# Decaying keys and queries in place by block exponents in a chunk-free gated linear attention, with operand packing and mask conversion on other engines

## The chip, the cores and the metric

One core of a Trainium2 chip runs the whole layer as one program. The engines have queues of their own, worked in order: PE (matmul), DVE (vector), ACT (scalar), POOL (GpSimd), and SP, which issues DMAs; POOL and ACT issue DMAs too. The metric is the device time of one execution in microseconds. The kernel before has a median of 878.82 us over three runs (877.24, 878.82, 879.69).

## The reference

A decoder layer on 512 tokens of width 1024: gated linear attention (GLA, 4 heads, keys of 128, values of 256) and multi-head latent attention (MLA, 8 heads) side by side, merged by gates, then an MLP of width 4096. Each half ends in a layer norm. All in float32. What the change touches is the GLA core, here as a recurrence over tokens t, for one head:

```
log_a = log_sigmoid(a_lr @ w_gla_a2 + b_gla_a2) / 16
b     = cumsum(log_a)                            # along the tokens, per channel d
score[i, j] = sum_d q[i, d] * k[j, d] * exp(b[i, d] - b[j, d])     for j <= i
o[i]  = sum_j score[i, j] * v[j]
```

The reference does this in chunks of 64 with a carried state; the result is the same lower triangle of scores over all 512 tokens.

## The kernel before

All matmuls of float32 operands are split in a high and a low part (`split`, and `pump` for weights at L199 and L200): ACT rounds the high part, DVE subtracts it from the source to get the low part, and PE runs three products (hi hi, hi lo, lo hi). Weights come through SP's queue as `wraw`, some through POOL's queue as `wq` with an accumulating DMA. PE is fed by long GEMM loops; between their steps `tick` advances small generators (`active`), whose instructions so fall between the matmuls. A scheduler in the tile framework then orders each engine's queue by its own timing model; `issue_after` pins an instruction behind another.

The order of the work around the change: input layer norm (`ln_in0`, `ln_in1`), the latent projections, `prep` (rope tables and masks), `gemm_fm` for q and k, `latents` (the gate logs GL, one tile per head, channels on partitions, tokens along the row) and `latents2` (RMS norm, transposes), `proj_v(0)`, `proj_r`, `proj_v(1)`, then the gates. From `proj_v(0)` on two generators run beside: `lane_levels` (`gla_levels` for each head) and `lane_out` (`gla_out`).

`gla_levels` builds the triangle of scores by levels s = 1, 2, 4, ..., 256. At level s the tokens are cut in blocks of 2s; the left half's keys meet the right half's queries. A key is decayed to the end of its half, a query from the start of its half. The tokens of the second 256 run backwards, so that `halves` gives left halves of one half and right halves of the other in one view. The steps before:

- `rp` holds two running sums for a head, R (for keys, zero at the start) and G (a copy of GL). `advance(s)` (L846, L847) adds, on POOL, the last value of the neighbour half to the halves: two additions of 128x256 a level.
- `vec(s)` takes E = exp(R / 16) and exp(G / 16) on ACT (L861, two a level), and multiplies them on DVE with the original keys and queries into M (L862, two a level).
- level 1 is done with the diagonal: `q1` (L883), `xs` (L887, L888), four products 192 wide (L897), then L905 (diagonal by the identity) and L906 (predicated copy of level 1).
- L912, L916 and L920 are the matmuls of the levels up to 64, of 128 and of 256, on M. `take` writes a level's scores into SD under a mask (L872, `copy_predicated`); the two largest levels are split for PE directly.
- at the end sd is split, its low part on POOL (L930).

The masks `lmask` are bytes, made by 14 casts on DVE (L566) from the integer tiles `lmi`; the second of these is loaded by `lm_load`: a memset on POOL and seven DMAs in POOL's queue. GL gets its last subtraction on POOL (L657). `ev_k` moves k from PSUM on DVE (L590), and `rms_T` scales the latents on DVE (L607). `latents` also casts aT (L634), which PE needs for the gate logits z (L639); `h_early` adds hraw (L1149).

Of the kernel before, what the change touches and what calls it, by code (L numbers as in the profile page):

```python
# [52 lines left out]
def tile_hybrid_block(ctx: ExitStack, tc: tile.TileContext, I, out, dbg=None):  # L53
# [45 lines left out]
        return bass.AP(tensor=ap.tensor, offset=ap.offset + step * (n - 1), ap=dims[:-1] + [[-step, n]])  # L99

    def view(ap, off, *dims):
        return bass.AP(tensor=ap.tensor, offset=ap.offset + off, ap=[list(ap.ap[0])] + [list(d) for d in dims if d[1] > 1])

    act = nc.scalar.activation
    vtt = nc.vector.tensor_tensor
# [332 lines left out]
    def ln_rows(src, dst, mv, on_act=False, behind=None):  # L438
        bst = S([P, 2, 6], F32, "bst")
        for j in range(2):  # L440
            with ExitStack() as gates:
                if j and behind is not None:
                    gates.enter_context(tc.issue_after(behind.ins))
                nc.vector.bn_stats(bst[:, j, :], src[:, j * T:(j + 1) * T])
        nc.vector.bn_aggr(mv, bst)
        vts(mv[:, 1:2], mv[:, 1:2], LN_EPS, None, op0=ALU.add)  # L446
        gtt(mv[:, 1:2], mv[:, 1:2], mhalf[:, 0:1], op=ALU.pow)  # L447
# [75 lines left out]
    def prep():  # L523
        with tc.issue_after(last_in.ins):
            vts(hbg, bgt, 0.5, None, op0=ALU.mult)
        posf = consts.tile([P, NT], F32, name="posf")
        with tc.issue_after(last_in.ins):
            nc.vector.tensor_copy(posf, posi)
        yield
        p = PX()  # L530
        nc.tensor.transpose(p[:2, :P], posf[:, 2:], identJ)
        nc.tensor.transpose(p[:, P:2 * P], masks[:, P:2 * P], ident)
        pr = B([2, P], F32, "pr")
        nc.vector.tensor_copy(pr, p[:2, :P])
# [24 lines left out]
        yield  # L559
        act(sn, angs[0], AF.Sin)  # L560
        act(cs, angs[1], AF.Sin)
        yield
        for s in LEVELS:
            for d in range(2):
                src = lmi[d][:, LEVELS.index(s), ::s]
                nc.vector.tensor_copy(lm(s)[:, d], src[:, None].to_broadcast([P, 2, 64 // s]))  # L566
        yield


# [17 lines left out]
        act(QK[a][:, 1, :], ps, AF.Copy, scale=P ** -0.5)  # L587

    def ev_k(a, ps):
        nc.vector.tensor_copy(QK[a][:, 0, :], ps)  # L590

    qlT, ckT, qld, ckd, GL, KKs = [], [], [], [], [], []
    aT = B([80, T], F32R, "aT")
# [2 lines left out]
    def rms_T(c0, n, g, outs, rest):  # L596
# [7 lines left out]
        gtt(rs, ss, mhalf[:, :NT], op=ALU.pow)  # L604
        yield
        for tt in range(NT):
            vts(lat[tt][:, c0:c0 + n], lat[tt][:, c0:c0 + n], rs[:, tt:tt + 1], None, op0=ALU.mult)  # L607
        yield
        for k in range(n // P):
            p = PX()  # L610
# [11 lines left out]
    def latents():  # L622
# [31 lines left out]
                last = act(azs[h], azs[h], AF.Ln, bias=1.0)  # L654
        t_ln[0] = last
        for h in range(GH):
            gtt(GL[h], GL[h], azs[h], op=ALU.subtract)  # L657
        yield

    def latents2():  # L660
# [25 lines left out]
        KKs.append(KK)  # L686


    def halves(v, s, right, off=0):

        if s >= P:
            return view(v, off + s * right, (256, T // (2 * s)), (1, s))
        return view(v, off + s * right, (256 - s if right else 256 + s, 2), (2 * s, P // s), (1, s))

    def last(v, s, right):

        if s >= P:
            return view(v, 2 * s - 1 if right else s - 1, (129, T // (2 * s))).to_broadcast([P, T // (2 * s), s])
        o = view(v, 2 * s - 1 if right else s - 1, (257 - 2 * s if right else 257, 2), (2 * s, P // s))
        return o[:, :, :, None].to_broadcast([P, 2, P // s, s])  # L700

    Vh = [[] for _ in range(GH)]
# [130 lines left out]
    def gla_levels(h):  # L833
        qk = QK[h]
        QK[h] = None
        rp = A([P, 2, T], F32, "rp")
        act(rp[:, 1, :], GL[h], AF.Copy)
# [5 lines left out]
        R, G = rp[:, 0, :], rp[:, 1, :]  # L843

        def advance(s):
            gtt(halves(R, s, 0), halves(R, s, 0), last(G, s, 1), op=ALU.add)  # L846
            gtt(halves(G, s, 1), halves(G, s, 1), last(G, s, 0), op=ALU.add)  # L847

        def vec(s):
            E = B([P, T], F32, "E")  # L850
            M = B([P, T], F32, "M")
            for w, src in enumerate((R, G)):
                if s >= P:
                    e, m = [v[:, 256 * w:256 * w + 256].rearrange("p (d i) -> p d i", i=s) for v in (E, M)]
                    if s == 256:
                        e, m = e[:, 0], m[:, 0]
                elif w:
                    e, m = [v[:, 256:].rearrange("p (d n i) -> p d n i", d=2, i=s) for v in (E, M)]
                else:
                    e, m = [v[:, :256].rearrange("p (n d i) -> p d n i", d=2, i=s) for v in (E, M)]  # L860
                act(e, halves(src, s, w), AF.Exp, scale=1.0 / 16.0)  # L861
                vtt(m, e, halves(qk[:, w, :], s, w), op=ALU.mult)  # L862
            if s < 256:
                advance(s)
            return M

        def take(s, p):
# [14 lines left out]
        q1 = B([P, NT, 64], F32, "q1")  # L882
        act(q1.rearrange("p (d t) n -> p d (t n)", d=2), halves(G, 1, 1), AF.Exp, scale=1.0 / 16.0)  # L883
        xs = [B([P, 2, 192], F32, "x1") for _ in range(2)]
        for i in range(2):
            t2 = slice(2 * i * P, 2 * (i + 1) * P)
            act(xs[i][:, :, :P], qk[:, 1, t2].rearrange("p (t i) -> p t i", i=P), AF.Copy)  # L887
            vtt(xs[i][:, :, P:], q1[:, 2 * i:2 * i + 2, :],  # L888
                qk[:, 1, t2].rearrange("p (t n two) -> p t n two", t=2, two=2)[:, :, :, 1 - i], op=ALU.mult)
        advance(1)  # L890
        yield
        px1 = []
        for i in range(2):
            p = PX()
            for t in range(2):
                c = slice((2 * i + t) * P, (2 * i + t + 1) * P)
                mm(p[:, t * 192:(t + 1) * 192], qk[:, 0, c], xs[i][:, t, :], start=True, stop=True)  # L897
            px1.append(p)
        s = 2
        M = vec(2)  # L900
        yield
        for i, p in enumerate(px1):
            pt = p[:, :384].rearrange("p (t c) -> p t c", c=192)
            d = SD[:, 2 * i:2 * i + 2, :]
            vtt(d, pt[:, :, :P], ident[:, None, :].to_broadcast([P, 2, P]), op=ALU.mult)  # L905
            nc.vector.copy_predicated(d.rearrange("p t (n two) -> p t n two", two=2)[:, :, :, 1 - i], lm(1)[:, i], pt[:, :, P:])  # L906
        prev = None
        while s < T:
            p = PX()
            if s <= 64:  # L910
# [14 lines left out]
            if s < T:  # L925
                M = vec(s)
# [820 lines left out]
```

## Time and profile before

| | |
|---|---|
| median of three runs | 878.82 us |
| profiled execution, its own time | 878.11 us |
| its span in the profile | 876.3 us |
| PE busy | 852.6 us (97%), 4711 records |
| DVE busy | 648.5 us (74%), 1093 |
| ACT busy | 470.4 us (54%), 830 |
| POOL busy | 198.6 us (23%), 235 |
| granted PE clock, mean | 0.998 |
| DMA moved | 134.79 MB, mean 154 GB/s |

Busy times count what an engine executes, not register, branch, semaphore or DMA-issuing instructions. Matmuls overlap, so a busy PE can still be a little below its peak. A row of the groups view gives line, engine, operation, output tile and input tiles, shape and count, then the busy time and the mean of one, then the idle time of that engine just before them and what ended it. A row of the waits view gives who waited, for whom, and the sum, the count and the longest.

### The profile page before, as it was taken

The numbers are of one execution on the slowest core, as the hardware profiler recorded it, in microseconds if no ns is written. First come the engines' busy times: TensorE is split into PE (matmuls) and PEld (weight loads), VectorE is DVE, ScalarE is ACT, GpSimd is POOL, SyncE is SP. The second block draws the span as 40 slices with busy tenths as digits, with TensorE's granted clock in tenths as the row PEclk, the third lists the DMA queues.
The fourth block names the chain that finished last, engine by engine and source line by source line (L and its number), as shares of the span: only waits on it lengthen the run. The fifth ranks groups of instructions, "written<-read, shape, count | busy, mean of one in ns | idle before, by whom it ended". The sixth has DMA issues, their size and how long they took to land.

```text
span 876.3 us, 12888 instructions
## 1 busy us (share of the span) xinstructions
PE 852.6 (97%) x4711; PEld 745.0 (85%) x4711; DVE 648.5 (74%) x1093; ACT 470.4 (54%) x830; POOL 198.6 (23%) x235
## 2 busy tenths in 40 slices
PE   5999999999999999999999999999999999999996
PEld 5987887879999978888888889988888888889985
DVE  7869989989665646757876888986567556787865
ACT  5456766756466634436655414576357446666820
POOL 1333536755201030300000013004400520141000
PEclk9999999999999999999999999999999999999999
DMA  7986936694748453322127436007932890499312
GB/s 244 277 190 173 341 121 152 207 264 158 190 115 203 127 149 102 103 65 73 57 83 262 160 121 240 1 1 212 275 90 46 261 246 24 92 238 227 122 61 79
DMA packets 95727, 134.79 MB, mean 154 GB/s; under 512 B 13073, under 2 KB 58564, under 8 KB 95664
## 3 DMA queue, kind: packets, MB, share of 16 engines
q1 hardware_dynamic: 73840, 92.36, 33.1%
q0 software_dynamic: 19616, 37.95, 20.2%
q10 hardware_dynamic: 2208, 3.66, 1.2%
q8 instruction: 37, 0.61, 0.3%
q14 instruction: 26, 0.21, 0.1%
HBM read 110.35 MB, written 8.91 MB: 136 GB/s over the span
## 4 chain that ended last, share of the span: by engine, by line
PE 86%; DVE 8%; DMA 3%; issue 1%; ACT 1%; POOL 0%; POOLq 0%; SPq 0%; DVEq 0%; ACTq 0%
PE mm L255 10%; PE mm L256 10%; PE mm L257 10%; PE mm L291 5%; PE mm L290 4%; PE mm L289 4%; PE mm L1268 4%; PE mm L1266 4%; PE mm L1267 4%; PE px L1556 2%; PE px L1557 2%; PE px L1555 2%; DVE M L862 2%; PE mm L1556 2%; PE mm L1557 2%; PE mm L1555 2%
## 5 line engine op out<-in xcount | busy, mean ns | idle before, releaser
L200 DVE TENSOR_TENSOR wlo<-wraw,whi 128x1024 fp32r<-128x1024 f32 (+1 forms) x102 | 100.5, 994 | 78.1 <-ACT whi L199 73.9
L199 ACT ACTIVATE whi<-wraw 128x1024 fp32r<-128x1024 f32 (+1 forms) x102 | 86.5, 860 | 86.1 <-PE mm L256 47.7
L256 PE MATMUL mm<-h,whi 128*128 128x512 f32 x224 | 87.2, 389 | 0.0
L255 PE MATMUL mm<-h,whi 128*128 128x512 f32 x224 | 87.1, 390 | 0.0
L257 PE MATMUL mm<-h,wlo 128*128 128x512 f32 x224 | 83.3, 390 | 1.6 <-DVE wlo L200 1.6
L1574 POOL DMA_DIRECT2D res<-ev x42 | 36.9, 1007 | 179.1 <-ACT ev L1572 147.8
L200 DVE TENSOR_TENSOR wlo<-wq,whi 128x1024 fp32r<-128x1024 f32 x44 | 55.1, 1252 | 28.1 <-ACT whi L199 28.1
L199 ACT ACTIVATE whi<-wq 128x1024 fp32r<-128x1024 f32 x44 | 46.5, 1057 | 28.9 <-PE mm L1267 20.3
L257 PEld LDWEIGHTS mm<-h,wlo 128*128 128x128 f32 x224 | 42.0, 188 | 10.6 <-DVE wlo L200 2.0
L1268 PE MATMUL mm<-sh,wlo 128*128 128x256 f32 x176 | 50.0, 284 | 0.0
L1267 PE MATMUL mm<-sh,whi 128*128 128x256 f32 x176 | 49.9, 283 | 0.0
L1266 PE MATMUL mm<-sh,whi 128*128 128x256 f32 x176 | 49.9, 283 | 0.0
L256 PEld LDWEIGHTS mm<-h,whi 128*128 128x128 f32 x224 | 42.1, 188 | 8.7
L255 PEld LDWEIGHTS mm<-h,whi 128*128 128x128 f32 x224 | 42.1, 188 | 8.7
L199 ACT ACTIVATE xh<-wraw 128x1024 fp32r<-128x1024 f32 (+1 forms) x28 | 27.2, 985 | 28.4 <-PE mm L291 16.2
L447 POOL TENSOR_TENSOR mv<-mv,mhalf 128x1 f32<-128x1 f32 x4 | 4.7, 1180 | 158.1 <-DVE mv L446 158.1
L862 DVE TENSOR_TENSOR M<-E,qk 128x256 f32<-128x256 f32 x64 | 37.6, 616 | 0.2 <-ACT E L861 0.2
L200 DVE TENSOR_TENSOR xl<-wraw,xh 128x1024 fp32r<-128x1024 f32 (+1 forms) x28 | 31.3, 1127 | 8.8 <-ACT xh L199 8.8
L1620 ACT ACTIVATE relu<-mm 128x512 f32<-128x512 f32 x24 | 14.1, 595 | 41.9 <-PE mm L257 41.9
L846 POOL TENSOR_TENSOR rp<-rp 128x256 f32<-128x256 f32 x32 | 30.3, 946 | 24.8 <-ACT E L861 15.1
L1028 POOL DMA_DIRECT2D QS<-q x32 | 16.0, 507 | 85.1 <-DMA wraw<-in_w_o_gla_dram 48.5
L861 ACT ACTIVATE E<-rp 128x256 f32<-128x256 f32 x64 | 25.8, 418 | 16.4 <-POOL rp L846 9.3
(489 smaller groups left out, 2805.8 us busy)
## 6 DMA issues: line engine op xcount, KB each, us to landing
wraw<-in_w_ff_dram SPq DMA_DIRECT2D x36, 512.0 KB, 5.0
wraw<-in_w_in_dram SPq DMA_DIRECT2D x30, 512.0 KB, 4.8
wq<-in_w_ff_dram POOLq DMA_DIRECT2D x26, 512.0 KB, 9.5
res<-ev POOLq DMA_DIRECT2D x42, 256.0 KB, 10.0
wq<-in_w_in_dram SPq DMA_DIRECT2D x20, 512.0 KB, 6.9
wq<-in_w_in_dram POOLq DMA_DIRECT2D x18, 512.0 KB, 9.5
hsd<-hs SPq DMA_DIRECT2D x16, 256.0 KB, 4.4
xr<-hsd SPq DMA_DIRECT2D x16, 256.0 KB, 4.3
```

The lines of the kernel that those rows point to most:

```text
L199: st["ins"] = act(hi[:, k, :n], raw[:, k, :n], AF.Copy)
L200: st["lo"] = vtt(lo[:, k, :n], raw[:, k, :n], f(hi[:, k, :n]), op=ALU.subtract)
L255: mm(o, hi[:, c], xh, start=first, stop=False)
L256: mm(o, hi[:, c], xl, start=False, stop=False)
L257: mm(o, lo[:, c], xh, start=False, stop=last)
L289: mm(o, xh, hi[:, :n], start=opens, stop=False, skip_group_check=share)
L291: mm(o, xl, hi[:, :n], start=False, stop=last, skip_group_check=share)
L862: vtt(m, e, halves(qk[:, w, :], s, w), op=ALU.mult)
L1266: mm(oa, hi[:, k, c], xh, start=opens and k == 0 and a == 0, stop=False, skip_group_check=True)
L1267: mm(oa, hi[:, k, c], xl, start=False, stop=False, skip_group_check=True)
L1268: mm(oa, lo[:, k, c], xh, start=False, stop=k == 3, skip_group_check=True)
L1574: nc.gpsimd.dma_start(res[tt + t][:, j * T:(j + 1) * T], e, accum_op=ALU.add)
```

## The change

- `gla_levels` keeps no running sums. e1 = exp(GL / 16). The sums of GL over blocks of 2, 4, ..., 256 tokens come from seven halving additions on DVE (256, 128, ..., 4 columns), and one exponential e2 over all of them. K (the tile of the keys itself) and Q (a new tile, q times e1) are decayed in place: at each level ACT copies the left halves of K and the right halves of Q into M, and DVE multiplies these same halves in K and Q by the block exponents of the neighbour half, repeated along the block by the view `across`.
- Level 1 runs as a level like the others (`vec(1)`), and the diagonal is a product of 128 columns by itself, masked by the identity in one operation. At level 128 the matmul reads K and Q directly, and ACT scales one block of each in place for level 256, which reads them directly too.
- Moved: the low part of sd and the subtraction of GL from POOL to DVE; the evacuation of k and the scaling of the latents from DVE to ACT; the mask casts from DVE to POOL, behind the last layer-norm power there; `lm_load` to the front of `prep`.
- `halves` and `view` lose the cases that are no longer used; `last` goes.

The core of the diff:

```diff
     def prep():
         with tc.issue_after(last_in.ins):
             vts(hbg, bgt, 0.5, None, op0=ALU.mult)
+        lm_load()
+        last_pow = st["pow"]
...
-        lm_load()
-        yield
...
-                nc.vector.tensor_copy(lm(s)[:, d], src[:, None].to_broadcast([P, 2, 64 // s]))
+                with tc.issue_after(last_pow.ins):
+                    nc.gpsimd.tensor_copy(lm(s)[:, d], src[:, None].to_broadcast([P, 2, 64 // s]))
...
     def ev_k(a, ps):
-        nc.vector.tensor_copy(QK[a][:, 0, :], ps)
+        act(QK[a][:, 0, :], ps, AF.Copy)
...
-            vts(lat[tt][:, c0:c0 + n], lat[tt][:, c0:c0 + n], rs[:, tt:tt + 1], None, op0=ALU.mult)
+            act(lat[tt][:, c0:c0 + n], lat[tt][:, c0:c0 + n], AF.Copy, scale=rs[:, tt:tt + 1])
...
-            gtt(GL[h], GL[h], azs[h], op=ALU.subtract)
+            vtt(GL[h], GL[h], azs[h], op=ALU.subtract)
...
+    def across(e, s, right):
+        o = view(e, 1 - right, (256 // s + 1 if right else 256 // s - 1, 2), (2, P // s))
         return o[:, :, :, None].to_broadcast([P, 2, P // s, s])
...
     def gla_levels(h):
-        rp = A([P, 2, T], F32, "rp")
-        act(rp[:, 1, :], GL[h], AF.Copy)
-        nc.gpsimd.memset(rp[:, 0, :], 0.0)
+        K, Q = qk[:, 0, :], B([P, T], F32, "QD")
+        e1, sums, e2 = [B([P, T], F32, n) for n in ("e1", "sums", "e2")]
...
-        def advance(s):
-            gtt(halves(R, s, 0), halves(R, s, 0), last(G, s, 1), op=ALU.add)
-            gtt(halves(G, s, 1), halves(G, s, 1), last(G, s, 0), op=ALU.add)
+        def of(v1, v2, s):
+            return v1 if s == 1 else v2[:, T - 1024 // s:T - 512 // s]
...
         def vec(s):
-            E = B([P, T], F32, "E")
             M = B([P, T], F32, "M")
...
-                act(e, halves(src, s, w), AF.Exp, scale=1.0 / 16.0)
-                vtt(m, e, halves(qk[:, w, :], s, w), op=ALU.mult)
-            if s < 256:
-                advance(s)
+            e = of(e1, e2, s)
+            act(M[:, :256].rearrange("p (n d i) -> p d n i", d=2, i=s), halves(K, s, 0), AF.Copy)
+            vtt(halves(K, s, 0), halves(K, s, 0), across(e, s, 0), op=ALU.mult)
+            act(M[:, 256:].rearrange("p (d n i) -> p d n i", d=2, i=s), halves(Q, s, 1), AF.Copy)
+            vtt(halves(Q, s, 1), halves(Q, s, 1), across(e, s, 1), op=ALU.mult)
             return M
...
+        act(e1, GL[h], AF.Exp, scale=1.0 / 16.0)
+        for s in (1, 2, 4, 8, 16, 32, 64):
+            v = of(GL[h], sums, s).rearrange("p (n two) -> p n two", two=2)
+            vtt(of(None, sums, 2 * s), v[:, :, 0], v[:, :, 1], op=ALU.add)
+        act(e2[:, :T - 4], sums[:, :T - 4], AF.Exp, scale=1.0 / 16.0)
+        vtt(Q, qk[:, 1, :], e1, op=ALU.mult)
+        p = PX()
+        for tt in range(NT):
+            c = slice(tt * P, (tt + 1) * P)
+            mm(p[:, c], qk[:, 0, c], qk[:, 1, c], start=True, stop=True)
+        M = vec(1)
+        yield
+        vtt(SD, p.rearrange("p (t c) -> p t c", c=P), ident[:, None, :].to_broadcast([P, NT, P]), op=ALU.mult)
...
             elif s == 128:
                 for i in range(2):
-                    mm(p[:, i * P:(i + 1) * P], M[:, i * P:(i + 1) * P],
-                       M[:, 256 + i * P:256 + (i + 1) * P], start=True, stop=True)
+                    mm(p[:, i * P:(i + 1) * P], K[:, 2 * i * P:(2 * i + 1) * P],
+                       Q[:, (2 * i + 1) * P:(2 * i + 2) * P], start=True, stop=True)
+                e = of(e1, e2, s)
+                act(K[:, :P], K[:, :P], AF.Copy, scale=e[:, 1:2])
+                act(Q[:, 3 * P:], Q[:, 3 * P:], AF.Copy, scale=e[:, 2:3])
             else:
                 for j in range(2):
-                    mm(p[:, j * 256:(j + 1) * 256], M[:, j * P:(j + 1) * P], M[:, 256:], start=True, stop=True)
+                    mm(p[:, j * 256:(j + 1) * 256], K[:, j * P:(j + 1) * P], Q[:, 256:], start=True, stop=True)
+            if s < 64:
+                M = vec(2 * s)
...
         act(sd[:, 0], SD, AF.Copy)
-        gtt(sd[:, 1], SD, f(sd[:, 0]), op=ALU.subtract)
+        vtt(sd[:, 1], SD, f(sd[:, 0]), op=ALU.subtract)
```

More of the change, by code (lines that the diff above doesn't have):

```diff
@@ L101, in view @@
     def view(ap, off, *dims):
-        return bass.AP(tensor=ap.tensor, offset=ap.offset + off, ap=[list(ap.ap[0])] + [list(d) for d in dims if d[1] > 1])
+        return bass.AP(tensor=ap.tensor, offset=ap.offset + off, ap=[list(ap.ap[0])] + [list(d) for d in dims])
     act = nc.scalar.activation
@@ L446, in ln_rows @@
         vts(mv[:, 1:2], mv[:, 1:2], LN_EPS, None, op0=ALU.add)
-        gtt(mv[:, 1:2], mv[:, 1:2], mhalf[:, 0:1], op=ALU.pow)
+        st["pow"] = gtt(mv[:, 1:2], mv[:, 1:2], mhalf[:, 0:1], op=ALU.pow)
         if on_act:
@@ L686, in latents2, with halves @@
         KKs.append(KK)
[L689 to L699, printed above, removed]
+    def halves(v, s, right):
+        return view(v, s * right, (256 - s if right else 256 + s, 2), (2 * s, P // s), (1, s))
+    def across(e, s, right):
+        o = view(e, 1 - right, (256 // s + 1 if right else 256 // s - 1, 2), (2, P // s))
         return o[:, :, :, None].to_broadcast([P, 2, P // s, s])
@@ L841, in gla_levels @@
         s128 = s256 = None
-        R, G = rp[:, 0, :], rp[:, 1, :]
-        def advance(s):
-            gtt(halves(R, s, 0), halves(R, s, 0), last(G, s, 1), op=ALU.add)
-            gtt(halves(G, s, 1), halves(G, s, 1), last(G, s, 0), op=ALU.add)
+        def of(v1, v2, s):
+            return v1 if s == 1 else v2[:, T - 1024 // s:T - 512 // s]
         def vec(s):
-            E = B([P, T], F32, "E")
             M = B([P, T], F32, "M")
[L852 to L862, printed above, removed]
-            if s < 256:
-                advance(s)
+            e = of(e1, e2, s)
[3 more added lines that the diff above has]
+            vtt(halves(Q, s, 1), halves(Q, s, 1), across(e, s, 1), op=ALU.mult)
             return M
@@ L879, in take @@
                 split(p.rearrange("p (a b) -> p a b", b=256), s256[:, 0], s256[:, 1])
[L882 to L890, printed above, removed]
-        yield
[L892 to L907, printed above, removed]
+        act(e1, GL[h], AF.Exp, scale=1.0 / 16.0)
[9 more added lines that the diff above has]
+        M = vec(1)
+        yield
+        vtt(SD, p.rearrange("p (t c) -> p t c", c=P), ident[:, None, :].to_broadcast([P, NT, P]), op=ALU.mult)
+        prev, s = None, 1
         while s < T:
@@ L924, in gla_levels @@
             s *= 2
-            if s < T:
-                M = vec(s)
             yield
```

## The prediction

> **What bounds the kernel now.** First the page's span line and the chain of waits, by engine.
>
> ```profile
> span 876.3 us, 12888 instructions
> ...
> PE 86%; DVE 8%; DMA 3%; issue 1%; ACT 1%; POOL 0%; POOLq 0%; SPq 0%; DVEq 0%; ACTq 0%
> ```
>
> The chain that ends last is 86% matmul; the next holder is DVE with 8%. The profiled execution took 878.11 us, so 1.8 us lie around its span. The median of the three runs is 878.82 us, 0.7 us above it. I sum against 878.1.
>
> Next the windows view, in three stages. Columns: stretch, length, busy time of PE, PEld, DVE, ACT and POOL, granted clock, DMA share, GB/s.
>
> ```profile
> 20.00:100.00 80.00, 77.55 (x405) 67.98 (x404) 63.95 (x149) 46.30 (x84) 28.61 (x28) 1.00 0.85 233
> 100.00:225.00 125.00, 121.14 (x665) 104.44 (x665) 114.21 (x194) 78.45 (x164) 72.72 (x78) 1.00 0.70 199
> 225.00:876.00 651.00, 643.21 (x3592) 563.13 (x3590) 456.28 (x721) 333.62 (x565) 94.93 (x121) 1.00 0.48 133
> ```
>
> The change touches only what runs before about 225 us. There PE is idle for 2.5 us (80 - 77.55) and 3.9 us (125 - 121.14): 6.3 us in all, the most that a faster helper engine can win. In the second stretch DVE is busy 114.2 of 125 us, 91%, and ACT only 78.5. So DVE is the engine that can be late. The waits view of PE from 20 to 230 us says who ended each idle time (sum, times, longest):
>
> ```profile
> PE mm L257 <- DVE wlo L200: 1.6, 1, 1.6
> PE mm L810 <- DVE wraw L200: 1.6, 1, 1.6
> PE mm L290 <- DVE wlo L200: 1.2, 1, 1.2
> PE px L639 <- DVE aT L634: 0.9, 1, 0.9
> PE px L912 <- DVE SD L872: 0.6, 2, 0.3
> PE px L912 <- DVE M L862: 0.5, 1, 0.5
> ```
>
> Sum 6.4 us, and every releaser is DVE. L639 and L257 wait before the GLA levels (2.5 us); the other 3.9 us lie inside them.
>
> **Why DVE is late.** Timeline rows: start, duration, engine and line, and in brackets the idle time before and its releaser.
>
> ```profile
> 56.65 0.23 DVE L566 CAST lmask<-lmi 128x128 uint8<-128x128 int32 x1 [5.12 <-DMA lmi<-in_c_lmask_dram]
> 56.93 3.72 POOL L750 DMA_DIRECT2D wq<-in_w_in_dram  x3 [3.47 <-PE mm L255]
> 57.47 0.47 PE L639 MATMUL px<-aT,wa 80*128 80x512 f32 x1 [0.90 <-DVE aT L634]
> 60.31 0.68 DVE L1149 TENSOR_TENSOR hraw<-h 128x512 f32<-128x512 f32 x1
> 68.30 3.50 DVE L1149 TENSOR_TENSOR hraw<-h 128x512 f32<-128x512 f32 x2
> 69.70 3.24 POOL L657 TENSOR_TENSOR g<-g,az 128x512 f32<-128x512 f32 x2 [0.16 <-ACT az L654]
> 71.72 2.31 DVE L200 TENSOR_TENSOR wlo<-wraw,whi 128x1024 fp32r<-128x1024 f32 x1
> 142.65 1.08 POOL L846 TENSOR_TENSOR rp<-rp 128x256 f32<-128x256 f32 x1
> 142.77 1.26 DVE L862 TENSOR_TENSOR M<-E,qk 128x256 f32<-128x256 f32 x1
> 149.10 0.50 DVE L862 TENSOR_TENSOR M<-E,qk 128x256 f32<-128x256 f32 x1
> ```
>
> Two things are to be seen. Until 56.65 the first mask conversion (L566) held DVE's queue for 5.12 us, waiting for a mask DMA; the cast aT behind it came late, and PE lost 0.9 us. The other: DVE operations stretch while POOL works: hraw takes 0.68 us alone and 1.75 beside the subtraction on POOL; the product M takes 0.50 us alone and 1.26 beside the running sum L846.
>
> [...]
>
> **The change, part by part.** Groups of instructions between 20 and 225 us: busy us, mean ns | idle before, releaser.
>
> ```profile
> L862 DVE TENSOR_TENSOR M<-E,qk 128x256 f32<-128x256 f32 x64 | 37.6, 616 | 0.2 <-ACT E L861 0.2
> L888 DVE TENSOR_TENSOR x<-q,qk 128x128 f32<-128x128 f32 x8 | 3.7, 496 | 0.0
> L906 DVE COPY_PREDICATED SD<-lmask,px 128x128 f32<-128x128 uint8 x8 | 3.4, 446 | 0.0
> L905 DVE TENSOR_TENSOR SD<-px,ca 128x256 f32<-128x256 f32 x8 | 3.1, 413 | 0.7 <-PE px L897 0.7
> L607 DVE TENSOR_SCALAR lat<-lat,rs 128x384 f32<-128x384 f32 (+1 forms) x8 | 2.8, 407 | 0.9 <-POOL rs L604 0.9
> L590 DVE COPY qk<-mm 128x512 f32<-128x512 f32 x4 | 2.7, 680 | 0.0
> L365 DVE TENSOR_TENSOR wq<-wq,wq 128x1024 f32<-128x1024 f32 x2 | 2.4, 1218 | 0.0
> L566 DVE CAST lmask<-lmi 128x128 uint8<-128x128 int32 (+6 forms) x14 | 1.7, 204 | 5.2 <-DMA lmi<-in_c_lmask_dram 5.1
> L668 DVE TENSOR_TENSOR kt<-lat,cs 128x64 f32<-128x64 f32 x4 | 0.8, 210 | 0.0
> L861 ACT ACTIVATE E<-rp 128x256 f32<-128x256 f32 x64 | 25.8, 418 | 16.4 <-POOL rp L846 9.3 <-POOL rp L847 7.0
> L601 ACT ACTIVATE sqj<-lat 128x384 f32<-128x384 f32 (+1 forms) x8 | 3.6, 466 | 0.0
> L887 ACT ACTIVATE x<-qk 128x256 f32<-128x256 f32 x8 | 2.9, 420 | 0.0
> L837 ACT ACTIVATE rp<-g 128x512 f32<-128x512 f32 x4 | 2.5, 631 | 0.0
> L587 ACT ACTIVATE qk<-mm 128x512 f32<-128x512 f32 x4 | 2.1, 590 | 0.0
> L846 POOL TENSOR_TENSOR rp<-rp 128x256 f32<-128x256 f32 x32 | 30.3, 946 | 24.8 <-ACT E L861 15.1 <-ACT rp L837 8.2 <-POOL rp L847 0.2
> L847 POOL TENSOR_TENSOR rp<-rp 128x256 f32<-128x256 f32 x32 | 29.0, 908 | 7.2 <-ACT q L883 2.7 <-ACT E L861 2.6
> ```
>
> *DVE.* Removed: L862, L888, L906, L905, L607, L590 and L566, together 55.0 us. Added for four heads: 56 products in place, at the 0.413 of L905, 23.1; four 512-wide products, four 512-wide diagonals, four subtractions for sd and four for GL, 16 at the 0.68 of L590, 10.9; the seven-step sums, at most two at 0.413 and five at 0.21 (L668) each, 1.9 per head, 7.5; one more predicated copy per head, at 0.446 to twice that, 1.8 at the most. Sum 43.3, so DVE loses 11.7 us of its own work. A price not in the trace is a product whose second operand repeats one element along a block; the nearest rows are 0.41 and 0.50, and I take 0.41 (at 0.50 the saving is 6.8). Also DVE no longer stretches beside POOL: the two hraw and the wlo around 70 us alone give back 3.50 - 1.36 and 2.31 - 1.22, 3.2 us.
>
> [...]
>
> *ACT.* Removed: L861, L887, L837, 31.2 us, and four exponentials of q1. Added: eight exponentials of 512 at 0.63, 5.0; 56 packing copies at 0.42, 23.5; eight scaled copies of 128 at no more than 0.42, 3.4; four evacuations of k at 0.59, 2.4; eight latent scalings at 0.47, 3.7. Sum 38.0: up to 7 us more. ACT had 46.5 us free of 125, and the 16.4 us that it waited for POOL (L861) go. I cost this at nothing: the cover is that free time. Without it, the evacuation of k is the first to hurt, because proj_v's accumulators wait for it: four at 0.59 are 2.4 us on PE. In the changed order the first two evacuations stand ahead of the latent scalings, so I expect cover.
>
> *POOL.* Removed: L846 and L847, 59.3 us, the memsets, and two kinds of subtraction. Added: 14 mask copies, between the 0.20 of L566 and the 0.95 of L846 each, 2.8 to 13.2 us; I take 0.4, nearer to L566, since both do the same work. The lmi DMAs move no further than past one weight DMA in POOL's queue, but the copies that wait for them stand ahead of four accumulating weight DMAs. Three of these start at 56.93 in the trace as well, held by PE (L750), about when the masks land (56.65); the fourth starts later than before, and its consumer is a product of proj_r, behind all of proj_v(0). I cost this at nothing.
>
> *PE.* Two rows of the groups over the whole span:
>
> ```profile
> L912 PE MATMUL px<-M 128*128 128x128 f32 x96 | 14.6, 278 | 1.1 <-DVE SD L872 0.6 <-DVE M L862 0.5
> L897 PE MATMUL px<-x,qk 128*128 128x192 f32 x32 | 6.0, 325 | 0.0
> ```
>
> L897 (32 records, 6.0 us) becomes 32 records 128 wide, and level 1 adds 16: 48 at 14.6/96 = 0.15 are 7.3. PE gets between 0 and 1.3 us more work, as records overlap; I take 0.5.
>
> *The path.* The 0.9 us at 57 goes wholly: nothing on DVE waits for the mask any more. At 72 to 74 us the subtraction of GL is now on DVE itself, one of the four (0.68) ahead of this wlo, against 3.2 us of stretching and 5 us of waiting saved; what is late next is whi, cast by ACT at about the same time, so I leave 0.4 of 1.6. Inside the levels 3.9 us go if DVE's load falls from 114 to about 100 of 121 us; PE then arrives 3 to 5 us sooner at whi casts and at weight DMAs that stand still, and I leave 1.2 for such new waits. Sum: -6.4 + 0.4 + 1.2 + 0.5 = -4.3 us: 878.1 - 4.3 = **873.8 us**.
>
> **Rivals.**
> 1. *Only the early part counts.* ACT's packing copies stand in ACT's queue between the whi casts, and whi takes the place of wlo as the wait inside the levels. For: both share one in-order queue, and ACT gets up to 7 us more. Against: ACT is 63% busy there (78.45 of 125). Time: 878.1 - 2.1 + 0.5 = 876.5.
> 2. *The level chain (slower).* A level's K product now waits for ACT's copy of the same halves, and the next copy waits for that product: the chain crosses two in-order queues with weight splits between. One step is 0.41 + 0.42, with one weight split on each 3.1 us (1.22 on DVE by L365; on ACT some 1.1, an estimate from the 0.63 of L837 for half the width). The tile view of M gives minimum/median/maximum ns, first and last start:
>
> ```profile
> L862 DVE TENSOR_TENSOR M<-E,qk x64: 401/506/1256, 101.9 to 216.2; 128x256 f32<-128x256 f32 x64
> ```
>
> So a head has 28.6 us (114.3 / 4), 3.2 per product of nine. With two DVE splits in one step it is 4.3, 1.1 us late, and PE's queue stands behind that product. Four of the 28 steps late so cancel the forecast's gain, more turn it; one in three, nine, with the waits inside the levels kept, gives 878.1 - 2.1 + 9 x 1.1 = 886. Against: two pairs (K and Q) are independent, and DVE's order puts at most one split in most steps.
> 3. *The mask copies on POOL.* At 0.95 each, they hold DVE 13 us between 20 and 100 us, where it is 80% busy (63.95 of 80). PE has only its two early waits there; if a third of the 13 reaches PE it costs 4 us: 878.1 - 4.3 + 4 = 878, no change.
>
> **How the numbers follow.** Forecast 0.64, rival 1 0.14, rival 2 0.12, rival 3 0.10. The forecast's own range is 871.0 (every wait gone, no new work, and the tails that overlap behind each wait) to 876.0. To leave out no more than 2 in 10, the range takes in rivals 1 and 3 and stops short of rival 2: 870.5 to 879.0. A measurement of this kernel tells 0.3%, 2.6 us, from no change. Faster by more (below 876.2): the forecast, a third of rival 1, and little of rival 3, 0.68. Within: 0.18. Slower: rival 2 and tails, 0.14.
>
> **What would show it.** PE's waits from 20 to 230 us should list no aT and no wraw row, and sum to 1 to 2.5 us. DVE's mean for the 128x256 products should be 0.40 to 0.45 with nothing above 0.6, and wlo L200 about 1.22. ACT's waits should no longer name POOL. A PE wait on M from ACT, or on whi, above 3 us in all would show rival 2 or 1; DVE operations above their free length beside a mask copy, rival 3. The forecast is wrong if PE's idle time before 225 us does not fall below 4 us.

## The result, and the profile after

The changed kernel takes 869.43 us (median of four runs, 869.17 to 870.49) against 878.26 us before (877.24 to 879.69): a ratio of 0.9901, 95% interval 0.9883 to 0.9918, or 8.8 us less. The forecast said 4.3 us less, 873.8, with 870.5 as its low end. The sign was right; the gain was twice as large, and the time lies below the range. The profiled execution took 869.47 us.

The span and the chain of waits by engine, from the page of the kernel after:

```profile
span 867.7 us, 12757 instructions
...
PE 97%; DMA 1%; DVE 1%; ACT 0%; POOLq 0%; issue 0%; DVEq 0%
```

The span fell by 8.6 us, and DVE's 8% of the chain became 1%. The same two stretches of the windows view (length, busy PE, PEld, DVE, ACT, POOL, clock, DMA share, GB/s):

```profile
20.00:100.00 80.00, 80.00 (x422) 70.61 (x421) 58.81 (x132) 49.64 (x90) 22.96 (x35) 1.00 0.87 240
100.00:225.00 125.00, 125.00 (x736) 110.67 (x735) 105.25 (x204) 81.63 (x172) 11.47 (x9) 1.00 0.71 205
```

PE is busy for all of 80 and all of 125 us, and gets through 88 more matmuls by 225 us (422 against 405, 736 against 665; 16 of them are new). The waits view of PE from 20 to 230 us has its two heading lines and no row under them:

```profile
core 0 of [0], span 867.7 us
engine line waited for: us in total, times, longest us
```

So all six waits of before are gone, and no new one came. Groups of DVE from 20 to 225 us that answer to those of before:

```profile
L200 DVE TENSOR_TENSOR wlo<-wraw,whi 128x1024 fp32r<-128x1024 f32 x24 | 29.4, 1227 | 10.9 <-ACT whi L199 10.9
L856 DVE COPY_PREDICATED SD<-lmask,px 128x256 f32<-128x256 uint8 x28 | 14.7, 524 | 3.0 <-PE px L883 2.7
L846 DVE TENSOR_TENSOR qk<-qk,e 128x256 f32<-128x256 f32 x28 | 11.8, 423 | 0.4 <-ACT M L845 0.2
L848 DVE TENSOR_TENSOR QD<-QD,e 128x256 f32<-128x256 f32 x28 | 11.8, 420 | 0.8 <-ACT M L847 0.7
...
L1123 DVE TENSOR_TENSOR hraw<-h 128x512 f32<-128x512 f32 x8 | 5.1, 683 | 0.0
L868 DVE TENSOR_TENSOR sums<-sums 128x128 f32<-128x128 f32 (+5 forms) x24 | 4.8, 201 | 0.7
...
L870 DVE TENSOR_TENSOR QD<-qk,e 128x512 f32<-128x512 f32 x4 | 2.7, 686 | 1.2 <-ACT e L865 1.2
...
L868 DVE TENSOR_TENSOR sums<-g 128x256 f32<-128x256 f32 x4 | 1.7, 418 | 0.0
```

One group of ACT, and one of POOL:

```profile
L845 ACT ACTIVATE M<-qk 128x256 f32<-128x256 f32 x28 | 11.7, 417 | 1.6 <-DVE qk L846 1.5
```

```profile
L567 POOL CAST lmask<-lmi 128x128 uint8<-128x128 int32 (+6 forms) x14 | 7.1, 788 | 3.8 <-DMA lmi<-in_c_lmask_dram 3.8
```

The 56 products in place take 0.42 us each, where the 64 products of before had a mean of 0.616. The additions of hraw fell from 0.959 to 0.683 with no edit to them; their row in the groups of before, from 20 to 225 us:

```profile
L1149 DVE TENSOR_TENSOR hraw<-h 128x512 f32<-128x512 f32 x8 | 7.3, 959 | 0.0
```

**What an idle row leaves out.** Two timeline rows of the kernel before, around its wait at 72 us, and two of the kernel after at the same place:

```profile
71.91 0.39 PE L255 MATMUL mm<-h,whi 128*128 128x512 f32 x1
72.14 0.39 PE L256 MATMUL mm<-h,whi 128*128 128x512 f32 x1
74.08 0.50 PE L257 MATMUL mm<-h,wlo 128*128 128x512 f32 x1 [1.56 <-DVE wlo L200]
```

```profile
72.06 0.39 PE L256 MATMUL mm<-h,whi 128*128 128x512 f32 x1
72.28 0.39 PE L257 MATMUL mm<-h,wlo 128*128 128x512 f32 x1
```

Without a wait the next matmul starts 0.23 us later, though one lasts 0.39: they overlap. In the kernel before L257 started 1.94 us after L256, so 1.71 us were lost, and the row in brackets says 1.56. A stall shorter than that overlap (0.39 - 0.23 = 0.16 us for these) leaves no idle time to list. I therefore add up, over all matmuls that start from 20 to 230 us, the time to the next one's start less the usual distance for that number of columns (0.229 us for 512, 0.165 for 360, 0.121 for 256, 0.163 for 192 and 0.112 for 128). I call this PE's loss: **9.35 us before, 0.76 after**, while the listed idle time went from 6.4 to 0. The difference of 8.59 us is the whole gain from the first matmul to the last (860.10 to 851.99 us from start to start, 8.1, with 0.16 us more matmul work and 0.3 elsewhere). The last 0.5 us of the span is a first matmul at 8.6 instead of 9.1 us; the transfers ahead of it, which the change does not touch, landed sooner (those of x of 512 KB took 4.5 us from issue to landing, 4.7 before). In the fourteen traces here that start lies between 8.3 and 9.1 us, with no tie to an edit, so these 0.5 us read as chance.

### The profile page after: what moved, and what is told of

It is laid out like the page before. It is cut to its first block, busy times and chain, and to the rows that moved or that the text cites. A ratio compares the mean times of both kernels' runs of the same rounds, so it can differ in the third digit from the quotient of the medians.

```text
span 867.7 us, 12757 instructions
## 1 busy us (share of the span) xinstructions
PE 851.0 (98%) x4727; PEld 746.0 (86%) x4727; DVE 630.3 (73%) x1083; ACT 473.4 (55%) x834; POOL 130.9 (15%) x173
## 4 chain that ended last, share of the span: by engine, by line
PE 97%; DMA 1%; DVE 1%; ACT 0%; POOLq 0%; issue 0%; DVEq 0%
PE mm L255 11%; PE mm L256 11%; PE mm L257 11%; PE mm L289 6%; PE mm L290 5%; PE mm L291 5%; PE mm L1242 4%; PE mm L1241 4%; PE mm L1240 4%; PE px L1530 3%; PE px L1531 3%; PE px L1529 3%; PE mm L1530 2%; PE mm L1531 2%; PE mm L1529 2%; PE mm L806 1%
## 5 line engine op out<-in xcount | busy, mean ns | idle before, releaser
L256 PE MATMUL mm<-h,whi 128*128 128x512 f32 x224 | 87.2, 389 | 0.0
L257 PE MATMUL mm<-h,wlo 128*128 128x512 f32 x224 | 83.2, 390 | 0.0
L256 PEld LDWEIGHTS mm<-h,whi 128*128 128x128 f32 x224 | 42.1, 188 | 8.7
L257 PEld LDWEIGHTS mm<-h,wlo 128*128 128x128 f32 x224 | 42.0, 188 | 8.7
L1594 ACT ACTIVATE relu<-mm 128x512 f32<-128x512 f32 x24 | 14.1, 596 | 42.0 <-PE mm L257 42.0
L1241 PEld LDWEIGHTS mm<-sh,whi 128*128 128x128 f32 x176 | 33.8, 192 | 0.0
L1242 PEld LDWEIGHTS mm<-sh,wlo 128*128 128x128 f32 x176 | 33.8, 192 | 0.0
L1240 PEld LDWEIGHTS mm<-sh,whi 128*128 128x128 f32 x176 | 33.8, 192 | 0.0
L1242 PE MATMUL mm<-h,wlo 128*128 128x256 f32 x112 | 32.1, 287 | 0.0
L1240 PE MATMUL mm<-h,whi 128*128 128x256 f32 x112 | 31.9, 285 | 0.0
```

Of the source, the lines that this page charges most:

```text
L256: mm(o, hi[:, c], xl, start=False, stop=False)
L257: mm(o, lo[:, c], xh, start=False, stop=last)
L1240: mm(oa, hi[:, k, c], xh, start=opens and k == 0 and a == 0, stop=False, skip_group_check=True)
L1241: mm(oa, hi[:, k, c], xl, start=False, stop=False, skip_group_check=True)
L1242: mm(oa, lo[:, k, c], xh, start=False, stop=k == 3, skip_group_check=True)
```

## The experiments

Two theories. A: DVE operations with two inputs in SBUF are stretched while POOL reads SBUF (the product M took 0.50 us alone and 1.26 beside a running sum); the change gains because POOL reads almost nothing any more. B: DVE simply has less work of its own. Ratios are to the kernel before in the same series; where two kernels are compared below by the ratios, the difference is that of their ratios times 878 us. "Product" is the mean of DVE's 128x256 products; the waits are PE's listed ones from 20 to 230 us, in us.

| kernel | median us | ratio (95%) | loss | waits | product |
|---|---|---|---|---|---|
| before | 878.26 | 1 | 9.35 | 6.4 | 0.616 |
| changed | 869.43 | 0.9901 (0.9883 to 0.9918) | 0.76 | 0 | 0.42 |
| e1 all edits outside the levels | 882.92 | 1.0051 (1.0039 to 1.0064) | 13.1 | 7.1 | 0.644 |
| e2 levels alone | 872.01 | 0.9937 (0.9924 to 0.9951) | 4.3 | 2.6 | 0.42 |
| e3 changed + POOL additions | 884.56 | 1.0069 (1.0056 to 1.0082) | 14.3 | 7.9 | 0.69 |
| e4 changed + POOL fills | 869.65 | 0.9905 (0.9890 to 0.9920) | 0.8 | 0 | 0.42 |
| e5 before, sums become fills | 872.52 | 0.9938 (0.9920 to 0.9956) | 4.4 | 2.0 | 0.425 |
| e6 before + mask + GL | 874.22 | 0.9957 (0.9943 to 0.9971) | 6.0 | 3.6 | 0.610 |
| e7 changed, packing on DVE | 877.11 | 0.9991 (0.9978 to 1.0003) | 9.5 | 5.3 | 0.42 |
| e8 e1, sums on DVE | 876.95 | 0.9991 (0.9979 to 1.0004) | 8.0 | 5.5 | 0.421 |
| e9 e6 + sd | 875.15 | 0.9960 (0.9948 to 0.9973) | 6.2 | 3.9 | 0.619 |
| e10 e6 + the ACT edits | 882.75 | 1.0044 (1.0032 to 1.0057) | 14.2 | 6.7 | 0.647 |
| e11 changed without sd and ACT edits | 869.92 | 0.9898 (0.9883 to 0.9913) | 1.0 | 0 | 0.42 |
| e12 e10, sums become fills | 870.03 | 0.9913 (0.9900 to 0.9927) | 0.85 | 0 | 0.426 |

For each of these kernels the loss above the changed kernel's 0.76 us gives its time above that kernel (by the ratios) to within 1.4 us.

**e1, the edits outside the levels.** Before, with `lm_load` at the front of `prep` and these lines of the change:

```diff
-                nc.vector.tensor_copy(lm(s)[:, d], src[:, None].to_broadcast([P, 2, 64 // s]))
+                with tc.issue_after(last_pow.ins):
+                    nc.gpsimd.tensor_copy(lm(s)[:, d], src[:, None].to_broadcast([P, 2, 64 // s]))
-            gtt(GL[h], GL[h], azs[h], op=ALU.subtract)
+            vtt(GL[h], GL[h], azs[h], op=ALU.subtract)
-        nc.vector.tensor_copy(QK[a][:, 0, :], ps)
+        act(QK[a][:, 0, :], ps, AF.Copy)
-            vts(lat[tt][:, c0:c0 + n], lat[tt][:, c0:c0 + n], rs[:, tt:tt + 1], None, op0=ALU.mult)
+            act(lat[tt][:, c0:c0 + n], lat[tt][:, c0:c0 + n], AF.Copy, scale=rs[:, tt:tt + 1])
-        gtt(sd[:, 1], SD, f(sd[:, 0]), op=ALU.subtract)
+        vtt(sd[:, 1], SD, f(sd[:, 0]), op=ALU.subtract)
```

> The kernel before with all edits outside the level loop: mask conversion on POOL, GL and sd subtractions on DVE, k evacuation and latent scaling on ACT. The running sums stay on POOL. Theory A (PE waited for a DVE that POOL's reads of SBUF stretch): the two waits ahead of the levels go (0.9 and 1.6 us idle, 2.5 to 2.8 us with the tails), those inside stay, since the products still lie beside the running sums: ratio 0.9965 to 0.9975, 875.2 to 876.1. Theory B (DVE had too much work of its own): 5.5 us of L590 and L607 leave DVE, 5.4 us of subtractions come; nothing inside changes much: 875 to 876 as well. DVE's 128x256 product stays at a mean near 0.62 us by both.

4.5 us slower instead of 2.5 faster: both theories missed. The early waits did go (PE busy 80.00 of 80 us); the waits from 100 us on, where the levels run, rose from 3.9 to 7.1 us, and the granted clock fell to 0.50 from 179.2 to 182.6 us. Which edit does it is asked in e6, e9 and e10.

**e2, the levels alone.** The changed kernel with the whole diff of e1 undone.

> The changed level loop alone; mask conversion, GL and sd subtractions, k evacuation and latent scaling as before. Theories A and B: the waits inside the levels go (3.9 us idle, some 5 us with tails), those at 57 and 74 us stay (2.5 to 2.8): ratio 0.9935 to 0.9950, 872.5 to 874. If e1 and e2 add up to the whole change (8.8 us) the parts are independent. If e2 alone gives over 7 us, the early waits were not worth what their rows say.

5.5 us faster by the ratio (6.0 by the medians). The two early waits stand as their rows said (1.6 and 1.0), and nothing waits inside the levels. The loss of the levels from 100 us on fell from 6.6 to 1.0 us. e1 and e2 do not add up to the change: +4.5 - 5.5 = -1.0, not -8.7. From this kernel to the changed one, the same outside edits take off 3.2 us.

**e3 and e4, POOL's reads put back, and fills in their place.** Both are the changed kernel with work on POOL behind each pair of products, into a tile that nothing reads. PE, DVE and ACT have the same order of instructions in the two.

```diff
             vtt(halves(Q, s, 1), halves(Q, s, 1), across(e, s, 1), op=ALU.mult)
+            for w in range(2):                                    # e3
+                gtt(junk[:, 256 * w:256 * w + 256], M[:, :256], M[:, 256:], op=ALU.add)
+            gtt(junk[:, :2], M[:, 0:2], M[:, 256:258], op=ALU.add)    # e4
+            for w in range(2):
+                nc.gpsimd.memset(junk, 0.0)
             return M
```

> The changed kernel with two additions 128x256 on POOL after each of the seven products pairs of a head, reading the packed operand M and writing a tile that nothing reads; 56 in all, about as many as the running sums had. DVE's own work and the chain between DVE and ACT stay as in the changed kernel. Theory A: DVE's products rise from 0.42 to 0.55 us or more in the mean, some of them past 1 us, and PE waits come back: 1.5 to 4 us over the changed kernel, 871 to 873.5. Theory B: products may stretch, but PE has room, since DVE has lost 12 us of work: within 0.7 us of the changed kernel (869 to 870.2).

> As the kernel with POOL additions, in the same order of instructions on every other engine, but POOL reads only 2 elements of M and then fills the unused tile twice (128x512 memsets that read nothing). Theory A, if reading SBUF is what stretches DVE: DVE's products stay at 0.42 to 0.45 us and the time is that of the changed kernel within 0.7 us. If writes stretch DVE as well, the products rise as with the additions. Theory B: no change in time either. So this one tells what POOL does to DVE; with the additions it forms a pair.

Of e3, the stretch of the levels in the windows view, then groups of DVE and of POOL, then in the timeline one weight split with the POOL row beside it:

```profile
100.00:225.00 125.00, 116.98 (x625) 98.59 (x624) 114.85 (x191) 74.87 (x157) 64.12 (x64) 0.97 0.66 184
```

```profile
L849 DVE TENSOR_TENSOR QD<-QD,e 128x256 f32<-128x256 f32 x28 | 19.7, 704 | 0.1
L847 DVE TENSOR_TENSOR qk<-qk,e 128x256 f32<-128x256 f32 x28 | 19.0, 679 | 0.5 <-ACT M L846 0.5
```

```profile
L851 POOL TENSOR_TENSOR junk<-M 128x256 f32<-128x256 f32 x56 | 55.2, 1015 | 52.9 <-ACT M L848 43.9 <-issue 8.6 <-POOL junk L851 0.4
```

```profile
140.68 3.48 DVE L200 TENSOR_TENSOR wraw<-wq,wraw 128x1024 fp32r<-128x1024 f32 x1
...
141.19 1.87 POOL L851 TENSOR_TENSOR junk<-M 128x256 f32<-128x256 f32 x2
```

The same three views of e4, windows, DVE and POOL:

```profile
100.00:225.00 125.00, 125.00 (x736) 110.42 (x735) 105.01 (x204) 81.52 (x171) 56.34 (x93) 1.00 0.71 204
```

```profile
L847 DVE TENSOR_TENSOR qk<-qk,e 128x256 f32<-128x256 f32 x28 | 11.8, 423 | 0.8 <-ACT M L846 0.5
```

```profile
L852 POOL MEMSET junk<- 128x512 f32 x56 | 29.9, 535 | 3.2
```

POOL is busy for 64 us of the 125 in e3 and 56 in e4. Where it reads, DVE's products go from 0.42 to 0.69 us, a split beside two additions takes 3.48 us (1.22 alone), and the kernel is 15 us slower than the changed one. Where it only fills, the products stay at 0.42 us and the time at 869.65. Theory A, and theory B falls with e3; but the size was put far too low (1.5 to 4 us). A part of the 15 us is the clock: in e3 it was 0.50 from 178.2 to 185.0 us, and 4.9 us of PE's loss of 14.3 lie there. Tiles held longer by POOL are not the cause: from 100 to 225 us no wait of PE, ACT or DVE in e3 names POOL.

**e5, the sums of the kernel before read nothing.** Each addition of `advance` becomes two fills; DVE keeps its 64 products.

```diff
-            gtt(halves(R, s, 0), halves(R, s, 0), last(G, s, 1), op=ALU.add)
-            gtt(halves(G, s, 1), halves(G, s, 1), last(G, s, 0), op=ALU.add)
+            for v, w in ((R, 0), (G, 1)):
+                for _ in range(2):
+                    nc.gpsimd.memset(halves(v, s, w), 0.0)
```

> The kernel before, with each running sum on POOL replaced by two fills of the same halves with zero: POOL works at the same places and ACT still waits for it, but POOL reads nothing. The level results are no longer the reference's (the decay by the running sums is left out). DVE keeps its 64 products and all else. Theory A (POOL's reads stretch DVE): the products fall from 0.62 to about 0.50 us and nothing is above 0.7, DVE is busy 100 to 105 of 125 us, and the waits inside the levels (3.9 us) fall below 1.5: 873.5 to 875.5. Theory B (12 us less work on DVE is what made the room): DVE keeps that work, so most of the waits stay: 876.5 to 878.5.

Theory A again, a little beyond its range: 5.4 us faster, no wait inside the levels. The levels alone (e2) gave 5.5, so taking POOL's reads away is worth as much as the whole change of the levels. (The two fills are also shorter than the addition that they replace, 0.6 us together against 0.9, so ACT gets its input a little sooner, and the order of the queues shifts in places. ACT still waits 9.7 us for POOL, 16.4 before; e3 against e4 is the pair with the same order, where only POOL's work differs.) The product's row in the groups of e5:

```profile
L863 DVE TENSOR_TENSOR M<-E,qk 128x256 f32<-128x256 f32 x64 | 24.9, 425 | 3.4 <-ACT E L862 3.3
```

0.425, not the 0.50 that I had taken for its free length: even the median product of the kernel before was stretched. The 64 products lose 12.2 us by POOL's reads.

**e6, mask and GL only; e9 and e10, the rest in two parts.** Of e1's diff, e6 has the mask and GL lines; e9 has these and the sd line; e10 has these and the two lines with `act` (k, latents).

> The kernel before with only the mask conversion on POOL (loads moved ahead) and the subtraction of GL on DVE. Its early waits (0.9 and 1.6 us) should go, as in the outside edits. Theory C, formed on the run with all outside edits (4.5 us slower): from 140 to 180 us DVE sets the pace, PE arrives 2.5 us sooner and waits that much longer there, and the bunched waits close the clock gate for some us: no gain, 877.5 to 880, PE's waits inside the levels 6 us or more, clock below 1.00 between 178 and 186 us. Rival: the slowdown came from the sd subtraction and the ACT edits, and these two alone give their 2.5 us: 875.5.

> The kernel before with mask conversion on POOL, GL subtraction on DVE and the sd subtraction on DVE; k evacuation and latent scaling stay on DVE. It is the 874.2 us kernel plus one edit; PE keeps its order. The kernel with all outside edits took 882.9, so sd, k evacuation and latent scaling cost 8.7 us together. Theory D: from 140 to 180 us DVE is 97% busy, so each us put on it there is lost on PE: two to four subtractions of 0.68 us, 1.4 to 2.7 us, 875.5 to 877. Theory E: the ACT edits, which change PE's order, cost the rest or all: then this one stays at 874 to 874.8.

> The kernel before with mask conversion on POOL, GL subtraction on DVE, k evacuation and latent scaling on ACT; the sd subtraction stays on POOL. Theory D: these edits take 5.5 us off DVE, so they cost nothing: 873 to 875. Theory E: they let the levels of a head start where other work of DVE is due, PE waits bunch up between 170 and 180 us and the granted clock falls after them: 879 to 883.

e6 is 3.8 us faster, so theory C falls: PE's time won early is not waited out later. PE's waits from 20 to 230 us are those of before, less the early two and one short one on SD:

```profile
PE mm L811 <- DVE wraw L200: 1.6, 1, 1.6
PE mm L290 <- DVE wlo L200: 1.2, 1, 1.2
PE px L913 <- DVE M L863: 0.5, 1, 0.5
PE px L913 <- DVE SD L873: 0.3, 1, 0.3
```

e9 costs 0.3 us over e6, which the intervals do not tell from nothing: DVE's busy time from 100 to 225 us rose by 3.1 us (112.89 to 115.95) and PE's loss by 0.2, so D falls. e10 costs 7.6 (E): edits that take work off DVE, with ACT busy for 77.5 of 125 us, make the kernel slower. They change the order of PE's and DVE's work; beside POOL's sums the products grow to 0.647 in the mean, and PE's waits bunch up. Windows of e10, and the first of these stretches in the kernel before:

```profile
174.00:178.00 4.00, 1.75 (x9) 1.19 (x10) 4.00 (x9) 3.17 (x6) 3.84 (x4) 1.00 1.09 348
178.00:180.00 2.00, 1.18 (x6) 0.48 (x4) 2.00 (x4) 0.24 (x1) 0.00 (x0) 0.58 1.09 349
180.00:182.00 2.00, 2.00 (x5) 1.61 (x6) 2.00 (x4) 0.00 (x0) 0.00 (x0) 0.50 1.18 242
182.00:184.00 2.00, 2.00 (x7) 1.52 (x6) 1.54 (x4) 0.00 (x0) 0.00 (x0) 0.50 1.23 226
```

```profile
174.00:178.00 4.00, 2.78 (x14) 1.89 (x14) 4.00 (x10) 2.23 (x5) 3.16 (x4) 1.00 1.09 349
```

After PE had been busy for 1.75 of 4 us the granted clock fell to 0.50, and stayed there until about 185 (windows of 1 us); with 2.78 of 4 it had stayed at 1.00. In those 6.8 us at half clock PE loses 3.4 us (0.5 in the same stretch of the kernel before), of which its listed waits hold 0.8.

**e7, packing on DVE.** Both packing copies of the changed kernel move from ACT to DVE; one of them:

```diff
-            act(M[:, 256:].rearrange("p (d n i) -> p d n i", d=2, i=s), halves(Q, s, 1), AF.Copy)
+            nc.vector.tensor_copy(M[:, 256:].rearrange("p (d n i) -> p d n i", d=2, i=s), halves(Q, s, 1))
```

> The changed kernel with the 56 packing copies on DVE in place of ACT. DVE gets some 20 us more work (56 at 0.35 to 0.42), ACT 23 us less. DVE was busy 105 of 125 us, so it would need all of the stage: PE waits of 3 to 10 us on M from DVE, 872 to 882. If the time stays within 0.7 us of the changed kernel, ACT's part was not needed.

7.9 us over the changed kernel, within the 872 to 882 expected, though a copy takes only 0.29 us on DVE (0.42 on ACT). PE's waits from 20 to 230 us in e7:

```profile
PE px L883 <- DVE M L847: 3.2, 1, 3.2
PE mm L806 <- DMA xr<-hsd: 2.1, 1, 2.1
```

ACT's share is needed: 16.4 us more on DVE takes most of the gain, by one long wait on M, one on a transfer that now comes late, and half clock from 160.7 to 167.5 us, behind the first of them.

**e8, the sums on DVE.** e1 with the additions of `advance` on DVE:

```diff
-            gtt(halves(R, s, 0), halves(R, s, 0), last(G, s, 1), op=ALU.add)
-            gtt(halves(G, s, 1), halves(G, s, 1), last(G, s, 0), op=ALU.add)
+            vtt(halves(R, s, 0), halves(R, s, 0), last(G, s, 1), op=ALU.add)
+            vtt(halves(G, s, 1), halves(G, s, 1), last(G, s, 0), op=ALU.add)
```

> The kernel before with the outside edits and the 64 running sums on DVE, none on POOL. The products fall to 0.50 us (8 us saved), the sums cost 64 x 0.41 to 0.50 = 26 to 32 us on DVE, ACT's waits for POOL go. DVE would need 130 us or more where PE has 121 us of work: 880 to 890, slower than with the sums on POOL (882.9) or about the same. If it comes out below 876, getting off POOL alone would have done.

A miss in the other direction: 5.3 us faster than e1, though DVE gets 26.8 us of sums. Two groups of its DVE, products and one of the two sums:

```profile
L863 DVE TENSOR_TENSOR M<-E,qk 128x256 f32<-128x256 f32 x64 | 26.8, 421 | 0.9 <-ACT E L862 0.9
L847 DVE TENSOR_TENSOR rp<-rp 128x256 f32<-128x256 f32 x32 | 13.4, 420 | 0.0
```

The products give 12.5 us of DVE's time back (39.3 to 26.8), a sum takes 0.42 where POOL took 0.9, and ACT gets its sums sooner. DVE is then too full (116.9 of 125 us) to beat the kernel before. Getting off POOL repairs the loss; doing so with fewer operations makes the gain.

**e11, without three edits; e12, the ACT edits without POOL's reads.** e11 is the changed kernel with the sd line and the two `act` lines of e1's diff undone (sd on POOL, k and latents on DVE). e12 is e10 with the diff of e5.

> The changed kernel without three of its edits: k evacuation and latent scaling on DVE and the sd subtraction on POOL, as before; the levels, the mask conversion and the GL subtraction stay changed. With the sums off POOL the order around them no longer matters if PE has no wait on DVE: within 0.7 us of the changed kernel (869 to 870.2). If DVE still was near the bound, 5.5 us of work more on it would bring waits back: 871 or more.

> The 882.8 us kernel (the kernel before with mask conversion on POOL, GL subtraction on DVE, k evacuation and latent scaling on ACT), with each running sum on POOL replaced by two fills that read nothing. The level results are no longer the reference's (the decay by the running sums is left out). If the ACT edits cost only because they shift DVE's products against POOL's reads (theory A with E), the cost goes with the reads: no PE wait between 20 and 230 us above 0.5, 868.5 to 871. If the ACT edits cost by ACT's own queue (copies ahead of weight rounding), they still cost when POOL reads nothing: 875 or more.

e11 equals the changed kernel: these three edits neither help nor harm there. e12 equals it too, with 64 products and 64 exponentials still in place (windows, then the group of the products):

```profile
100.00:225.00 125.00, 125.00 (x726) 110.75 (x725) 100.47 (x198) 83.23 (x178) 53.85 (x141) 1.00 0.73 204
```

```profile
L864 DVE TENSOR_TENSOR M<-E,qk 128x256 f32<-128x256 f32 x64 | 25.3, 426 | 6.9 <-ACT E L863 6.9
```

So the 7.6 us of the ACT edits need POOL's reads beside them (the order of PE's work differs as well between e10 and e12, so how much of it is order alone stays open). And nearly all of the change's gain (7.6 of 8.7 us by the ratios, whose intervals overlap) comes with sums that read nothing and these outside edits, without one product less. None of these kernels beats the changed one; from 20 to 230 us PE's loss there is 0.76 us, and no idle time is listed.

## Why the prediction was half the size

The forecast was -6.4 of idle time, with 0.4, 1.2 and 0.5 given back: -4.3. Measured, from the same span: -8.59 of loss, +0.16 of matmul work, +0.3 elsewhere, -0.5 from the earlier first matmul: -8.6.

- **The 6.4 us of idle rows.** The step that failed most. "6.3 us in all, the most that a faster helper engine can win" took busy time for full speed. The loss was 9.35 us: the listed waits hold about 1 us more than their rows (stalls above 0.25 us sum to 7.4), and shorter stalls the other 1.9, of which the changed kernel keeps 0.76. The mis-sized term is worth 2.2 us.
- **"I leave 0.4 of 1.6" at 72 us and "I leave 1.2" inside the levels.** No wait came in their place: 1.6 us too much was given back. The casts of whi were not late next, and e6 shows that the early part alone gives 3.8 us (2.1 were forecast for it).
- **PE work, 0.5.** The 128-column products cost 0.16 us more than the 192-column ones. The earlier start, which reads as chance, less the 0.3 elsewhere, adds the rest of the 4.3 us missed.
- **DVE's work.** Products in place 0.42 (0.41 taken), 512-wide operations 0.686 (0.68), sums 6.5 us (7.5). The four added predicated copies stand at 0.524, 2.1 us; "1.8 at the most" was a slip, since four at 0.446 to twice that are 1.8 to 3.6. The weight splits stand at 1.227 (1.22 said). DVE's busy time from 20 to 225 us fell from 178.2 to 164.1, 14.1 us, against 11.7 + 3.2. But the split between the two was wrong: 0.50 was taken as the product's free length. At 0.425 the 64 products hold 12 us of stretch, and I counted stretch only around 70 us. With that seen, the room on DVE would have been put down to POOL's reads, not to fewer products.
- **ACT at nothing.** Its busy time rose by 6.5 us (up to 7 was said), and no ACT wait names POOL. Costing it at nothing was right for this change (PE has no listed wait left), but the reason given, ACT's free time, does not carry: with the same free time and POOL's reads beside, the two ACT edits cost 7.6 us (e10).
- **POOL's mask casts.** 0.51 us of busy time each (7.1 / 14; 0.4 was taken), within the bounds, and rival 3 did not come: DVE was not held. That a copy holds DVE for its own length was my estimate, and no run shows it. It was POOL's casts that took longer. Timeline rows of the kernel after, at two places where casts lie beside DVE, and between them one where DVE is idle:

```profile
23.88 2.95 POOL L567 CAST lmask<-lmi 128x128 uint8<-128x128 int32 x7
...
25.25 0.95 DVE L200 TENSOR_TENSOR xl<-wraw,xh 128x720 fp32r<-128x720 f32 x1
...
53.31 0.65 POOL L567 CAST lmask<-lmi 128x128 uint8<-128x128 int32 x3 [3.75 <-DMA lmi<-in_c_lmask_dram]
...
57.76 2.33 POOL L567 CAST lmask<-lmi 128x8 uint8<-128x8 int32 x3
...
58.32 1.28 DVE L1123 TENSOR_TENSOR hraw<-h 128x512 f32<-128x512 f32 x2
```

  The cast of 32 columns lasted 0.91 us beside the split of the second row, which kept about its usual 0.90, and 0.23 in the third row, with DVE idle. In the last pair casts of 8, 4 and 2 columns lasted 1.9 to 2.1 us each, while two hraw passed in 1.28, their free length; there two weight DMAs that POOL issues lie over the same time, so how much of it was DVE's doing stays open.
- **POOL's reads.** With POOL reading SBUF beside them DVE's products, which have both inputs there, took 0.69 us, and with POOL only filling 0.42 (e3, e4). e5 and e12, where the sums read nothing, have 0.425 and 0.426 against 0.616 (before) and 0.647 (e10). The predicated copies, whose scores lie in PSUM, stood at 0.518 us in e3 and 0.524 in the changed kernel. The prediction priced POOL's reads for the early waits and the mask casts. In the levels it saw them in one row (1.26 against 0.50) and put no price on them, though most of their effect lay there.
- **Rivals.** 1 (only the early part counts) fell by e2, where the levels alone give 5.5 us. 2 (the level chain) did not come: PE never waits on M. It needs DVE to be fuller: e7 shows such a wait, 3.2 us. 3 is told above.

## What to carry to other kernels

Price a helper engine by the minimum of its durations, not by the median: where the two differ something else may hold it (0.40 and 0.51 here, with a mean of 0.425 once POOL read nothing), and moving that something may be worth more than removing work. To see how much a matmul queue can win, compare the starts of its matmuls with their undisturbed distance; idle rows gave 6.4 of 9.35 us here. An edit's price belongs to the kernel around it: the same edits outside the levels cost 4.5 us with POOL's sums beside them and gave 3.2 without.

## What the runs showed of the hardware

- The clock fell to 0.50 without any long gap on PE: in e10 no idle time between 174 and 178 us was over 1.1 us, and PE was busy 44% of it (1.75 of 4 us); in e1 it was busy 49% of the time from 175 to 179 us (1.96 of 4). Half clock lasted some 6.8 us in e10, as in e3 and e7, and some 3.4 in e1. What sets these two lengths no run shows.
- Of DVE and POOL, now one took longer beside the other and now the other: a DVE split went from 1.22 to 3.48 us beside two additions on POOL (e3), and in the kernel after a POOL cast of 32 columns went from 0.23 to 0.91 us beside a DVE split of 0.95 (0.90 elsewhere).
